# Two one-column constants in one tile: all tile pools start 32 bytes lower in a two-layer fp32 trunk

## The chip, the core and the metric

The kernel runs on one core of one Trainium2 chip. The metric is the device time of one execution in microseconds (us), the median of the runs that are shown. All tensors are float32, and the matrix products are made from float32 operands split into two parts.

## What is computed

The reference is a decoder trunk of `DEPTH` = 2 layers over 256 tokens of width 1024. Each layer has three blocks, and each block ends in a layer norm:

```
x = layer_norm(ALPHA * x + 0.5 * swiglu(x, ffn_w1[l, 0], ffn_w2[l, 0]), ...)
mix = hybrid_mixer(x, w_in[l], ...)
x = layer_norm(ALPHA * x + mix, ...)
x = layer_norm(ALPHA * x + 0.5 * swiglu(x, ffn_w1[l, 1], ffn_w2[l, 1]), ...)
```

`swiglu` is `(silu(x @ w1_gate) * (x @ w1_up)) @ w2` with an inner width of 2816. `hybrid_mixer` makes one projection of x to seven blocks of 1024 columns, runs a gated short convolution and a gated linear recurrence on them, projects each of the two results with a 1024 x 1024 matrix, merges them with sigmoid gates and projects the sum once more. Two places need a constant that an instruction reads as a one-column operand: a square root in the recurrence (a bias of 1e-30) and the power -0.5 in the layer norm.

## The kernel before

**Matrix products.** Each weight arrives in units of 128 partitions x 2048 float32 columns (1 MB). `emit_unit` (L185 to L199) loads a unit into a `raw` tile with DMAs from SyncE's queue (L193), ScalarE rounds it to `hi` (L197), and VectorE makes `lo = raw - hi` (L198). Activations are split in the same way. A product is then three matmuls: high by high, high by low and low by high, all issued in `mm` (L202). There are 8,838 matmuls with as many weight loads. In TensorE's terms, the *stationary* operand (128 columns) is loaded ahead of a matmul by a weight load, and the *moving* operand (256 or 512 columns) is streamed through. The weight load of one matmul overlaps the matmul before it.

**Which operand comes from where.** This decides what the change moves, so here are the three kinds of matmul:

- 256 columns, moving operand in the tiles of x or y, stationary operand in a weight unit. `mm_cols` (L204 to L211) makes them: the gate and up projections of the feed-forward blocks (bank `gu`), the mixer's projections (`c`, `v`, `b`, `y`, `ga`, `gb`) from `xh` and `xl`, and the two output projections (`wc`, `wr`) from `yh` and `yl`.
- 512 columns, moving operand in a weight unit, stationary operand in `xh`/`xl` (the `fill` matmuls of `filler`, L304 to L314) or in `yh`/`yl` (part of the `acc` matmuls of `form_b`, L278 to L287).
- Both operands in tiles of a pool: the other `acc` matmuls (stationary operand in an activation slot; 512 columns, but 256 in the last half of the last block), and the `rg` matmuls (256 columns, L471 to L476).

**Where the tiles lie.** A tile takes the same range of bytes in every partition. The pool `const` comes first and is as large as the sum of its tiles; the pools `praw`, `phi`, `plo`, `act` and `small` follow. In `const`, after `ident` and `xtok`, lie `xh`, `xl`, `yh` and `yl` (8 rows of 256 float32: 8,192 bytes each), `gB` and `bB` (4,096 each), `vec` (832), `hbm` and `hrg` (128 each), `sp2` (64), `tiny` and `mhalf` (one column of 4 bytes, for which 32 bytes are set aside each), then `rows0` and `rows1` (512 each) and six tiles of the parameter set-up (64 each). The tiles of the weight pools take 8,192 bytes and those of `act` 2,048 bytes. Slices of these tiles that a matmul reads begin at multiples of 512 bytes inside them.

**Order of work.** The program is a list of steps made up front (L224 to L227) and issued by the loop at L603 to L616. Ahead of each step it emits weight units as long as no more than `LOOK` = 6 are outstanding beyond those freed. The two constants are written by VectorE at L597 and L598, ahead of everything else on that engine. `mhalf` is read by GpSimd at L260, once in each of the 12 layer norms; `tiny` is read by ScalarE at L501, eight times in the kernel.

Of the kernel before, what the change touches and what calls it, by code (L numbers as in the profile page):

```python
# [9 lines left out]
F32 = mybir.dt.float32  # L10
# [4 lines left out]
P = 128  # L15
# [23 lines left out]
def trunk_kernel(  # L39
# [33 lines left out]
    const = ctx.enter_context(tc.tile_pool(name="const", bufs=1))  # L73
# [29 lines left out]
    hbm = const.tile([P, DEPTH, 2 * KD], F32, name="hbm")  # L103
    hrg = const.tile([P, DEPTH, 2 * KD], F32, name="hrg")
    sp2 = const.tile([P, DEPTH, KD], F32, name="sp2")
    tiny = const.tile([P, 1], F32, name="tiny")

    mhalf = const.tile([P, 1], F32, name="mhalf")

    def load_x(hh):  # L110
        for t in range(NT):
# [534 lines left out]
```

## Time and profile before

| what | value |
|---|---|
| median of 3 runs (lowest to highest) | 1224.68 us (1224.0 to 1225.43) |
| the profiled execution's own time | 1224.83 us |
| its span in the profile | 1223.0 us |
| granted TensorE clock, mean | 0.999 |
| VectorE busy | 825.3 us (67%) |
| ScalarE busy | 591.1 us (48%) |
| GpSimd busy | 14.9 us (1%) |
| share of the 16 DMA engines that the weight queue took | 58.6% |

A row of the profile names the engine, the line of the kernel and the tiles (out<-in, without buffer numbers). PE is a matmul on TensorE, PEld a weight load, DVE is VectorE, ACT ScalarE, POOL GpSimd, and SPq the DMA-issuing queue of SyncE. Matmuls are pipelined, so the duration of one matmul is longer than the time from its start to the start of the next; the rate is read from starts, or from the length of a run of back-to-back matmuls divided by their count. The chain of waits is the work that ended last, followed back from the end, and in it a row has the start in us, the length in us and the count.

### The profile page before, as it was taken

What the parts mean: (1) busy time and instruction counts of PE and PEld (TensorE: products, weight loads), DVE (VectorE), ACT (ScalarE), POOL (GpSimd) and SP (SyncE); (2) the same over time, 40 slices, a digit from 0 to 9 for tenths busy, and PEclk for the clock granted to TensorE, in tenths of its full rate; (3) what the DMA queues carried; (4) which work ended last, traced back from release to release, by engine and by line L of the source; (5) the groups of instructions that cost most, each with busy time, mean ns of one, the idle gap of its engine ahead of it and who ended that gap; (6) DMA issues with size and microseconds to landing.
All of it is one profiled execution on the core that took longest, in us unless ns stands there. A gap on an engine that the chain in (4) does not pass through costs nothing.

```text
span 1223.0 us, 20210 instructions
## 1 busy us (share of the span) xinstructions
PE 1207.2 (99%) x8838; PEld 1132.5 (93%) x8838; DVE 825.3 (67%) x794; ACT 591.1 (48%) x572; POOL 14.9 (1%) x20
## 2 busy tenths in 40 slices
PE   7999999999999999999999999999999999999997
PEld 5999988999999889998889998889999998899996
DVE  5766546868997785654575654577699967756533
ACT  5544434576575354443254443265856743544420
POOL 0000000000000000000000000000000000000000
PEclk9999999999999999999999999999999999999999
DMA  9975555638565566565566555565475654755610
GB/s 314 290 228 205 181 198 172 222 121 264 188 203 178 170 224 211 188 205 176 168 223 211 187 206 175 170 224 189 141 250 196 201 179 154 259 185 195 202 40 35
DMA packets 184257, 236.30 MB, mean 193 GB/s; under 512 B 4248, under 2 KB 164200, under 8 KB 184168
## 3 DMA queue, kind: packets, MB, share of 16 engines
q1 hardware_dynamic: 184168, 235.00, 58.6%
q8 instruction: 69, 1.13, 0.4%
q14 instruction: 20, 0.16, 0.0%
HBM read 233.94 MB, written 1.05 MB: 192 GB/s over the span
## 4 chain that ended last, share of the span: by engine, by line
PE 98%; DVE 1%; ACT 0%; DMA 0%; issue 0%; SPq 0%; DVEq 0%; ACTq 0%
PE gu L202 32%; PE acc L202 23%; PE fill L202 11%; PE c L202 4%; PE v L202 4%; PE b L202 4%; PE wr L202 4%; PE gb L202 4%; PE y L202 4%; PE ga L202 4%; PE wc L202 4%; PE rg L202 2%; PE xT L237 1%; DMA raw<-in_ffn_w_dram 0%; PE x L420 0%; PE hT L361 0%
## 5 line engine op out<-in xcount | busy, mean ns | idle before, releaser
L198 DVE TENSOR_TENSOR lo<-raw,hi 128x2048 fp32r<-128x2048 f32 (+1 forms) x218 | 493.8, 2270 | 254.9 <-ACT hi L197 254.6
L197 ACT CAST hi<-raw 128x2048 fp32r<-128x2048 f32 (+1 forms) x216 | 410.1, 1906 | 413.1 <-issue 190.7
L202 PE MATMUL gu<-xh,hi 128*128 128x256 f32 x1152 | 154.8, 277 | 0.0
L202 PE MATMUL gu<-xh,lo 128*128 128x256 f32 x1152 | 154.3, 276 | 0.0
L202 PE MATMUL gu<-xl,hi 128*128 128x256 f32 x1152 | 154.3, 276 | 0.0
L202 PEld LDWEIGHTS gu<-xh,hi 128*128 128x128 f32 x1152 | 141.9, 188 | 0.3
L202 PEld LDWEIGHTS gu<-xl,hi 128*128 128x128 f32 x1152 | 141.6, 188 | 0.0
L202 PEld LDWEIGHTS gu<-xh,lo 128*128 128x128 f32 x1152 | 141.5, 188 | 0.0
L202 PE MATMUL acc<-hi,hl 128*128 128x512 f32 (+1 forms) x180 | 65.8, 366 | 0.0
L202 PE MATMUL acc<-hi,hh 128*128 128x512 f32 (+1 forms) x180 | 65.8, 366 | 0.0
L202 PE MATMUL acc<-lo,hh 128*128 128x512 f32 (+1 forms) x180 | 65.8, 365 | 0.0
L345 DVE TENSOR_TENSOR hv<-hv,gu 128x512 f32<-128x512 f32 x36 | 24.8, 688 | 48.9 <-PE gu L202 48.8
L202 PE MATMUL fill<-hi,xh 128*128 128x512 f32 x192 | 53.7, 403 | 3.4 <-DVE hi L197 2.1
L202 PE MATMUL fill<-hi,xl 128*128 128x512 f32 x192 | 52.8, 398 | 0.6 <-DVE xl L242 0.6
L202 PE MATMUL acc<-hi,yh 128*128 128x512 f32 (+1 forms) x144 | 53.0, 368 | 0.0
L202 PE MATMUL acc<-hi,yl 128*128 128x512 f32 (+1 forms) x144 | 52.9, 368 | 0.0
L202 PE MATMUL fill<-lo,xh 128*128 128x512 f32 x192 | 52.6, 396 | 0.0
L202 PE MATMUL acc<-lo,yh 128*128 128x512 f32 (+1 forms) x144 | 52.4, 364 | 0.0
L202 PEld LDWEIGHTS fill<-hi,xh 128*128 128x128 f32 x192 | 36.0, 192 | 13.3 <-ACT xh L241 4.4
L202 PEld LDWEIGHTS fill<-hi,xl 128*128 128x128 f32 x192 | 36.5, 191 | 9.2 <-DVE xl L242 1.4
L202 PEld LDWEIGHTS fill<-lo,xh 128*128 128x128 f32 x192 | 36.6, 191 | 8.1
L241 ACT CAST xh<-xT 128x512 fp32r<-128x512 f32 x24 | 13.5, 590 | 60.4 <-PE xT L237 60.0
(172 smaller groups left out, 1866.4 us busy)
## 6 DMA issues: line engine op xcount, KB each, us to landing
raw<-in_ffn_w_dram SPq DMA_DIRECT2D x116, 1024.0 KB, 5.1
raw<-in_w_in_dram SPq DMA_DIRECT2D x56, 1024.0 KB, 5.1
raw<-in_ffn_w_dram SPq DMA_DIRECT2D x28, 512.0 KB, 4.1
raw<-in_w_out_conv_dram SPq DMA_DIRECT2D x8, 1024.0 KB, 5.4
raw<-in_w_out_rnn_dram SPq DMA_DIRECT2D x8, 1024.0 KB, 5.3
raw<-in_w_o_dram SPq DMA_DIRECT2D x8, 1024.0 KB, 4.9
raw<-in_rg_w_dram SPq DMA_DIRECT2D x4, 1024.0 KB, 6.6
gB<-in_ln_g_dram SPq DMA_DIRECT2D x6, 512.0 KB, 5.6
```

The lines of the kernel that those rows point to most:

```text
L197: (nc.vector.tensor_copy if first else nc.scalar.copy)(hi[:, part], raw[:, part])
L198: nc.vector.tensor_sub(lo[:, part], raw[:, part], f(hi[:, part]))
L202: nc.tensor.matmul(ps, lhs, rhs, start=first, stop=last)
L237: nc.tensor.transpose(ps[:, i * P : (i + 1) * P], xtok[:, t, c * P : (c + 1) * P], ident)
L241: nc.scalar.copy(dh, v)
L345: nc.vector.tensor_mul(o, o, u)
```

## The change

The tiles `tiny` and `mhalf` become the two columns of one tile, `two`. The names `tiny` and `mhalf` now stand for one column each, and all instructions that write or read them stay as they are.

```diff
@@ -103,9 +103,8 @@
     hbm = const.tile([P, DEPTH, 2 * KD], F32, name="hbm")
     hrg = const.tile([P, DEPTH, 2 * KD], F32, name="hrg")
     sp2 = const.tile([P, DEPTH, KD], F32, name="sp2")
-    tiny = const.tile([P, 1], F32, name="tiny")
-
-    mhalf = const.tile([P, 1], F32, name="mhalf")
+    two = const.tile([P, 2], F32, name="two")
+    tiny, mhalf = two[:, 0:1], two[:, 1:2]
```

One tile of 8 bytes takes 32 bytes where two tiles took 64. So `const` is 32 bytes smaller, and what lies behind these tiles moves down by 32 bytes: the tiles `rows0`, `rows1` and those of the parameter set-up, and all tiles of the pools. `ident`, `xtok`, `xh`, `xl`, `yh`, `yl`, `gB`, `bB`, `vec`, `hbm`, `hrg` and `sp2` stay where they are. The program has the same instructions with the same shapes on the same engines in the same order.

## The prediction

> **What bounds the kernel now.** I read the page's busy times first, then the chain of waits, then who made TensorE wait.
>
> ```profile
> span 1223.0 us, 20210 instructions
> PE 1207.2 (99%) x8838; PEld 1132.5 (93%) x8838; DVE 825.3 (67%) x794; ACT 591.1 (48%) x572; POOL 14.9 (1%) x20
> ...
> PEclk9999999999999999999999999999999999999999
> ...
> PE 98%; DVE 1%; ACT 0%; DMA 0%; issue 0%; SPq 0%; DVEq 0%; ACTq 0%
> ```
>
> The chain is 98% matmuls, at a granted clock that never drops. The list of waits, for TensorE alone:
>
> ```profile
> PE xT L237 <- DMA xtok<-in_x_dram: 4.4, 1, 4.4
> PE fill L202 <- DVE hi L197: 2.1, 2, 1.4
> PE fill L202 <- ACT xh L241: 1.3, 5, 0.3
> PE fill L202 <- DVE xl L242: 0.6, 1, 0.6
> ```
>
> These are 8.4 us in all, 4.4 of them the first load of x. So only one thing can move the time by much: the interval from one matmul to the next. The chain in order of time gives it, as length by count:
>
> ```profile
> 35.56 5.65 PE gu L202 x48
> 41.22 0.87 PE hT L361 x8
> 42.09 16.97 PE gu L202 x144
> 59.24 76.20 PE gu L202 x672
> ...
> 196.76 11.01 PE fill L202 x48
> ...
> 220.63 5.66 PE c L202 x48
> ...
> 241.37 5.66 PE c L202 x48
> ...
> 304.64 21.76 PE wc L202 x192
> ...
> 821.99 5.66 PE c L202 x48
> ...
> 842.73 5.66 PE c L202 x48
> ```
>
> The reader should divide. Matmuls of 256 columns go at 21.76 us / 192 = 113.3 ns in `wc` and 76.20 / 672 = 113.4 in `gu`, but at 16.97 / 144 = 117.8 in `gu` just before, and 5.66 / 48 = 117.9 in the first `c`. They are the same instruction, shape and alignment; nothing waits. So there are at least two steady patterns of matmul and weight load, and which of them a stretch falls into depends on how it begins.
>
> The `fill` matmuls of 512 columns take 11.01 / 48 = 229.4 ns. Now three pairs of rows from the timeline of TensorE; each pair is the first and last of a run of equal matmuls:
>
> ```profile
> 136.42 0.39 PE L202 MATMUL acc<-lo,h0h 128*128 128x512 f32 x1
> ...
> 145.94 0.39 PE L202 MATMUL acc<-lo,h0h 128*128 128x512 f32 x1
> ```
>
> From start to start there are 42 matmuls: 9.52 us / 42 = 226.7 ns. Both operands are in pools.
>
> ```profile
> 176.22 0.39 PE L202 MATMUL acc<-hi,yh 128*128 128x512 f32 x1
> ...
> 178.97 0.39 PE L202 MATMUL acc<-hi,yh 128*128 128x512 f32 x1
> ```
>
> Here 12 matmuls take 2.75 us, 229.2 ns each. The stationary operand is in `yh` and `yl`, the moving one in a pool.
>
> ```profile
> 1157.43 0.28 PE L202 MATMUL acc<-lo,h0h 128*128 128x256 f32 x1
> ...
> 1159.95 0.28 PE L202 MATMUL acc<-lo,h0h 128*128 128x256 f32 x1
> ```
>
> These are 21 matmuls of 256 columns in 2.52 us: 120.0 ns each, both operands in pools. The same shape with the moving operand in a tile of x takes 113.3.
>
> **What the addresses say.** From the start of `xh` to the first weight pool lie 4 x 8,192 + 2 x 4,096 + 832 + 2 x 128 + 64 + 2 x 32 + 2 x 512 + 6 x 64 = 43,584 bytes. That is 340 x 128 + 64. All slices and pool tiles step by multiples of 128 bytes, so any operand in a pool lies 64 bytes off any operand in `xh` to `yl`, modulo 128, and two operands in pools lie 0 off each other. Thus the trace before shows two distances: at 0, 256 columns take 120.0 ns and 512 take 226.7; at 64, 256 columns take 113.3 (sometimes 117.8) and 512 take 229.2 to 229.4. The distance is what I hold responsible; operand size, engine and clock are equal in each pair. After the change the distance from x or y to a pool is 43,552 bytes, 340 x 128 + 32. Two operands in pools stay at 0. No row shows a distance of 32. This is the unknown, bounded by rows on both sides.
>
> A rule of the Trainium skill speaks against all this: in "SBUF — State Buffer", section "Who interferes with whom", TensorE has two independent read ports, one for the moving operand and one for weight loads, and never waits on anyone. By it the distance does not matter and the change is worth 0. The trace does not agree: 120.0 against 113.3 ns for one shape.
>
> **Part by part.** *The constants.* Their instructions stay:
>
> ```profile
> L597 DVE MEMSET tiny<- x1: 59/59/59, 0.8 to 0.8; 128x1 f32 x1
> ...
> L598 DVE MEMSET mhalf<- x1: 59/59/59, 0.8 to 0.8; 128x1 f32 x1
> ...
> L260 POOL TENSOR_TENSOR rs<-rs,mhalf x12: 912/917/982, 189.3 to 1217.4; 128x1 f32<-128x1 f32 x12
> ```
>
> Both writes end before 1 us, under TensorE's wait of 4.4 us for x. Afterwards the tile is only read, so a shared tile gives no reader a new wait. Cost 0; without that cover, 0.12 us.
>
> *The 256-column matmuls with x or y moving.* Their counts, by form:
>
> ```profile
> L202 PE MATMUL gu<-xh,hi 128*128 128x256 f32 x1152 | 154.8, 277 | 0.0
> ...
> L202 PE MATMUL c<-xh,hi 128*128 128x256 f32 x128 | 17.8, 281 | 0.0
> ```
>
> `mm_cols` makes three forms of each, and the mixer has eight kinds like `c` with 128 of each form: 3 x 1,152 + 8 x 3 x 128 = 6,528 matmuls, about 740 us, over half the kernel. Upper bound: all go at the 120.0 of distance 0. About 384 already go at 117.8 (48 + 144 at the first `gu`, and four stretches of 48 `c`, by the rows of the chain above). So it is 6,144 x 6.7 + 384 x 2.2 = 42 us. At 117.8 for all it is 6,144 x 4.5 = 27.6 us. Lower bound: the 384 settle at 113.3, which gives -1.7 us. Below 113.3 I know no row of this shape, and 256 against 512 columns in their best patterns, 113.3 against 226.7, scale exactly with the columns: this looks like the stream's own rate, not a collision. I take 0. My reason is that a matmul at distance 64 has already found a pattern without loss, and half of the shift away from it need not lose it; but 32 lies as near to 0 as to 64, so this is weakly held.
>
> *The 512-column matmuls with x or y stationary.*
>
> ```profile
> L202 PE MATMUL fill<-hi,xh 128*128 128x512 f32 x192 | 53.7, 403 | 3.4 <-DVE hi L197 2.1 <-ACT xh L241 1.3
> ...
> L202 PE MATMUL acc<-hi,yh 128*128 128x512 f32 x112 | 44.1, 394 | 0.0
> ```
>
> Three forms of each: 576 + 336 = 912. At the distance-0 rate they would give back 576 x 2.7 + 336 x 2.5 = 2.4 us; at today's rate 0. A worse pattern, say as much again as today's loss, costs 2.4. Halfway between the two known distances I take half of the gain, -1.2 us.
>
> *Pool with pool.* The distance stays 0: cost 0. These operands also move by 32 bytes themselves, but so far a run follows the distance; nothing in the trace prices it.
>
> *ScalarE, VectorE and the DMAs* read and write the moved tiles.
>
> ```profile
> L198 DVE TENSOR_TENSOR lo<-raw,hi 128x2048 fp32r<-128x2048 f32 (+1 forms) x218 | 493.8, 2270 | 254.9 <-ACT hi L197 254.6
> L197 ACT CAST hi<-raw 128x2048 fp32r<-128x2048 f32 (+1 forms) x216 | 410.1, 1906 | 413.1 <-issue 190.7
> ...
> 60.00:135.00 75.00, 75.00 (x664) 75.00 (x663) 47.54 (x54) 32.81 (x30) 2.92 (x1) 1.00 0.63 211
> ...
> raw<-in_ffn_w_dram SPq DMA_DIRECT2D x116, 1024.0 KB, 5.1
> ```
>
> In 75 us of `gu`, VectorE is busy for 47.54, ScalarE for 32.81 and the DMA engines for 0.63 of the time. A unit feeds 48 matmuls, 5.44 us, against 2.27 us of subtraction. If they became 5% slower it would stay under the matmuls; uncovered are only the 4.0 us for which `fill` waits, so 0.2 us. I take 0.
>
> **Sum.** 1224.83 (the profiled execution, span 1223.0 and 1.8 around it) - 1.2 = 1223.6 us. The execution lies 0.15 above the median, which I neglect.
>
> **Rivals.**
>
> *Lost pattern (slower).* At 32 bytes off, weight loads and moving streams meet as at 0 bytes. For it: the 120.0 ns rows; the 117.8 ns stretches, which show that even at 64 the good pattern is not the only one. Against: most of the kernel holds 113.3 after many different starts. Price 42 - 2.4 (the 512 columns then go at 226.7) = 39.6: 1264.4 us; with the milder pattern 27.6: about 1252. It decides from 0.4 ns per matmul, since 6,528 x 0.38 is 2.45 us.
>
> *All patterns settle (faster).* Both small losses vanish: -2.4 - 1.7 = -4.1, 1220.7 us. For it: the 512 columns are better at 0 than at 64, so 64 is not the best distance for them. Against: at 0 the 256 columns are worst.
>
> *The stream gets faster than 113.3.* The eight `hT` transposes above take 0.87 / 8 = 109 ns each with a full weight load, so weight loads allow 109. If the change freed the stream to that rate, 6,528 x 4.3 = 28 us: 1196.8. Against: the exact scaling with columns. The Trainium skill, "TensorE: Matmul & The Clock Gate", section "Wait — 56ns, not 53.3ns?", gives columns / 2.4 GHz + 2.5 ns from start to start, an estimate of 109.2 ns for 256 columns; the trace has 113.3 at a clock of 0.999.
>
> *Nothing at all.* Independent reads, as the first rule has it: 1224.8 us. Against: the pairs of rows.
>
> **How the numbers follow.** Forecast 0.36 (1222.4 to 1226), nothing at all 0.05, lost pattern 0.33 (about half of it at the full price), all settle 0.21, a faster stream 0.05. A measurement of this kernel can tell 0.2%, 2.45 us, from no change. Faster: 0.21 + 0.05 = 0.26; within: 0.36 + 0.05 = 0.41; slower: 0.33. The range leaves out the faster stream and the last microseconds beyond the full price: 1220.0 to 1265.0. The likeliest case's own range is 1222.4 to 1226.
>
> **What would show it.** Right: `wc` stays at 21.76 us for 192 and the later `gu` at 113.4 ns; `acc` with `yh` falls between 226.7 and 229.2; the list of TensorE's waits stays near 8.4 us. A lost pattern would show as 192 `wc` in 22.6 to 23.0 us with no new wait. `fill` at 226.7 and the first `gu` at 113.3 would show that all settled. The prediction is wrong if time moves while all these intervals stand, for then it is no matter of matmul patterns.

## The result, and the profile after

The changed kernel takes 1260.4 us (median of 4 runs, 1259.39 to 1260.81) against 1225.03 us for the kernel before on the same chip: ratio 1.0281, 95% interval 1.0263 to 1.03. It is slower by 35.4 us. The span of the profiled execution grows from 1223.0 to 1259.0 us.

First the page of the changed kernel: busy times, granted clock, and the engines' shares of the chain.

```profile
span 1259.0 us, 20210 instructions
PE 1243.2 (99%) x8838; PEld 1163.9 (92%) x8838; DVE 826.0 (66%) x794; ACT 590.5 (47%) x572; POOL 14.9 (1%) x20
...
PEclk9999999999999999999999999999999999999999
...
PE 98%; DVE 1%; DMA 0%; ACT 0%; issue 0%; SPq 0%; DVEq 0%; ACTq 0%
```

The instruction counts are the same, the clock is the same, and VectorE, ScalarE and GpSimd are busy for the same time as before within 1 us. Only TensorE's busy time is longer, by 36 us, which is the whole difference of the spans. Next, the list of waits for TensorE:

```profile
PE xT L236 <- DMA xtok<-in_x_dram: 4.2, 1, 4.2
PE fill L201 <- DVE hi L196: 2.3, 2, 1.6
PE fill L201 <- ACT xh L240: 1.3, 5, 0.3
PE fill L201 <- DVE xl L241: 0.6, 1, 0.6
```

These are 8.4 us, as before: no engine and no load makes TensorE wait longer. So the time lies between matmuls that wait for nothing. The chain in order of time (start, length, count):

```profile
43.49 17.03 PE gu L201 x144
60.71 79.54 PE gu L201 x672
...
202.05 11.21 PE fill L201 x48
...
226.32 5.68 PE c L201 x48
...
312.96 22.72 PE wc L201 x192
```

Divide again. `wc` goes at 22.72 us / 192 = 118.3 ns per matmul (113.3 before), `gu` at 79.54 / 672 = 118.4 (113.4), `fill` at 11.21 / 48 = 233.5 (229.4). The first `gu` and the first `c`, which went at 117.8 and 117.9 before, go at 118.3 too. The timeline of TensorE has the other kinds, first and last row of a run:

```profile
180.64 0.40 PE L201 MATMUL acc<-hi,yh 128*128 128x512 f32 x1
...
183.44 0.40 PE L201 MATMUL acc<-hi,yh 128*128 128x512 f32 x1
...
1192.95 0.28 PE L201 MATMUL acc<-hi,h0h 128*128 128x256 f32 x1
...
1195.35 0.28 PE L201 MATMUL acc<-lo,h0h 128*128 128x256 f32 x1
```

With a stationary operand in `yh` and `yl`, 12 matmuls take 2.80 us, 233.3 ns each (229.2 before). With both operands in pools, 20 matmuls of 256 columns take 2.40 us, 120.0 ns each, as before.

The sum: 6,144 matmuls of 256 columns that went at 113.4 lose 5.0 ns, 30.7 us; the 384 others lose 0.5, 0.2 us; `fill` loses 576 x 4.2 ns, 2.4 us; `acc` on y loses 336 x 4.1, 1.4 us. The 96 `acc` matmuls of 256 columns with a stationary operand in `yh` or `yl`, in the last block, stand neither in the list of kinds above nor in the prediction's counts; they go from 113.6 to 117.4 ns on average, 0.4 us. That is 35.1 of the 36.0 us of the spans. Another 1.0 us lies in the first 20 `fill` matmuls, which follow the first loads: 7.73 us by the chain, 6.69 before. They took 7.48 in the first experiment below, where all distances are as before, so that is not shown to be an effect of the change.

### The profile page after: what moved, and what is told of

Read it like the earlier page. It is cut to its first block, busy times and chain, and to the rows that moved or that the text cites. A ratio compares the mean times of both kernels' runs of the same rounds, so it can differ in the third digit from the quotient of the medians.

```text
span 1259.0 us, 20210 instructions
## 1 busy us (share of the span) xinstructions
PE 1243.2 (99%) x8838; PEld 1163.9 (92%) x8838; DVE 826.0 (66%) x794; ACT 590.5 (47%) x572; POOL 14.9 (1%) x20
## 4 chain that ended last, share of the span: by engine, by line
PE 98%; DVE 1%; DMA 0%; ACT 0%; issue 0%; SPq 0%; DVEq 0%; ACTq 0%
PE gu L201 32%; PE acc L201 23%; PE fill L201 11%; PE c L201 4%; PE v L201 4%; PE b L201 4%; PE gb L201 4%; PE y L201 4%; PE ga L201 4%; PE wc L201 4%; PE wr L201 4%; PE rg L201 2%; PE xT L236 1%; DMA raw<-in_ffn_w_dram 0%; PE hT L360 0%; PE x L419 0%
## 5 line engine op out<-in xcount | busy, mean ns | idle before, releaser
L197 DVE TENSOR_TENSOR lo<-raw,hi 128x2048 fp32r<-128x2048 f32 (+1 forms) x218 | 493.8, 2270 | 272.3 <-ACT hi L196 272.2
L201 PE MATMUL gu<-xh,hi 128*128 128x256 f32 x1152 | 160.2, 281 | 0.0
L201 PE MATMUL gu<-xl,hi 128*128 128x256 f32 x1152 | 159.8, 281 | 0.0
L201 PE MATMUL gu<-xh,lo 128*128 128x256 f32 x1152 | 159.8, 281 | 0.0
L201 PEld LDWEIGHTS gu<-xh,hi 128*128 128x128 f32 x1152 | 146.7, 188 | 0.4
L201 PEld LDWEIGHTS gu<-xl,hi 128*128 128x128 f32 x1152 | 146.5, 188 | 0.0
L201 PEld LDWEIGHTS gu<-xh,lo 128*128 128x128 f32 x1152 | 146.5, 188 | 0.0
```

The costliest lines, as they stand in the source:

```text
L197: nc.vector.tensor_sub(lo[:, part], raw[:, part], f(hi[:, part]))
L201: nc.tensor.matmul(ps, lhs, rhs, start=first, stop=last)
```

## The experiments

From here on, the *distance* is the place of the stationary operand minus that of the moving one, in bytes of a partition, modulo 256 (the runs show below that 256 is the period). All distances are worked out from the sizes and the order of the tiles in the program; no trace here lists addresses. For the 256-column matmuls that stream x or y the distance is 64 before and 32 after. For the 512-column ones the roles are exchanged, so it is -64 (192) before and -32 (224) after. All kernels but the two that change `mm_cols` have the same instructions in the same order on every engine. The rows under each experiment are from the chain in order of time.

**Theory:** the interval of a matmul follows the distance of its own two operands. **Rivals:** the shared tile costs; or what counts is where a tile itself begins.

### Sharing without the shift

```diff
     two = const.tile([P, 2], F32, name="two")
+    gap = const.tile([P, 1], F32, name="gap")
```

> The constants share a tile, and an unused tile of 32 bytes behind it puts the pools back: distance of a pool from x and y 64 modulo 128. Distance theory: as before, 1224.7 us, wc at 113.3 ns per matmul. Rival, the shared tile itself costs (its readers or writers wait): as after, 1260 us.

Measured: 1224.73 us, ratio 0.9997 (0.9986 to 1.0009).

```profile
59.69 76.20 PE gu L202 x672
...
197.20 11.01 PE fill L202 x48
...
305.09 21.76 PE wc L202 x192
```

These three are the lengths of before to the last digit. The shared tile costs nothing; the 32 bytes account for the whole loss.

### Everything 32 bytes higher

```diff
+    gap = const.tile([P, 8], F32, name="gap")
     ident = const.tile([P, P], F32, name="ident")
```

> The kernel before with an unused tile of 32 bytes ahead of everything: x, y and all pools move up by 32 bytes, the pools now begin at 96 modulo 128 instead of 64, and the distance stays 64. Distance theory: 1224.7 us, wc at 113.3 ns. Rival, what counts is where a tile itself begins (a multiple of 64 bytes or not): 1260 us or more, since x and pools both lie 32 bytes off.

Measured: 1224.7 us, ratio 0.9998 (0.9984 to 1.0012).

```profile
196.32 11.01 PE fill L203 x48
...
304.39 21.76 PE wc L203 x192
```

Weights, slots, x and y all lie off a multiple of 64 bytes here, and nothing is lost. So 32 bytes more in the place of every operand do not matter to this kernel. That holds for the casts, the subtractions and the loads too, which work on the same moved tiles: a cast to `hi` takes 1,906 ns, a subtraction 2,270 ns and a 1 MB load of the feed-forward weights 5.1 us, in the kernel before and here.

### Pools 32, 64 and 128 bytes higher

```diff
     mhalf = const.tile([P, 1], F32, name="mhalf")
+    gap = const.tile([P, 8], F32, name="gap")    # 16 and 32 columns in the other two
```

> The kernel before with 32 bytes more ahead of the pools: distance 96 instead of 64. Distance theory: if 32 bytes more is the mirror image of 32 bytes less, as after, 118.3 ns for 256 columns and 233.3 for 512 with x or y stationary, 1260 us; if only the sense from moving to stationary counts, the two classes differ from after, and 256 columns lie between 113.3 and 120. Rival, where a tile itself begins: pools off a multiple of 64, 1260 us.

> The kernel before with 64 bytes more ahead of the pools: distance 0 modulo 128. Distance theory, by the pool-with-pool rows of before: 256 columns at 120.0 ns, 512 at 226.7, so 1264.4 us. Rival, where a tile itself begins: pools now at a multiple of 128, 1224.7 us or less.

> The kernel before with 128 bytes more ahead of the pools: distance 192 instead of 64, 64 modulo 128. Distance theory with a period of 128 bytes: as before, 1224.7 us, wc 113.3 ns and fill 229.4 ns per matmul. Rival, a longer period (512 bytes): other intervals, any time from 1222 to 1262 us.

Measured: 1258.24 us at distance 96, ratio 1.0266 (1.0244 to 1.0288); 1262.19 us at 128, ratio 1.0297 (1.0274 to 1.032); 1256.12 us at 192, ratio 1.025 (1.0235 to 1.0265). The three kernels in this order:

```profile
200.86 11.21 PE fill L203 x48
...
311.29 22.53 PE wc L203 x192
```

```profile
200.99 11.17 PE fill L203 x48
...
312.01 22.79 PE wc L203 x192
```

```profile
201.69 11.22 PE fill L203 x48
...
312.08 22.61 PE wc L203 x192
```

`wc` goes at 117.3, 118.7 and 117.8 ns, `fill` at 233.5, 232.7 and 233.8. The place of a tile is refuted once more, since at 128 and at 192 all pools begin at multiples of 64. But my own theory failed in part: I had taken 128 bytes for the period. Then 128 should have given `fill` the 226.7 of distance 0, and 192 should have been as good as 64. Neither is so.

### Distance 0, 320 and 256: the period

The first diff moves `sp2` (64 bytes) from behind the tiles of x and y to ahead of them; the second moves `hbm` and `hrg` (256 bytes), the third all three.

```diff
+    sp2 = const.tile([P, DEPTH, KD], F32, name="sp2")
     ident = const.tile([P, P], F32, name="ident")
...
-    sp2 = const.tile([P, DEPTH, KD], F32, name="sp2")
```

> The tile sp2 of 64 bytes moves ahead of everything: x and y lie 64 bytes higher, the pools stay, and the distance is 0 modulo 512 (in the run at distance 0 modulo 128 it was 128 modulo 512, and fill took 232.7 ns there, against 226.7 for two operands in pools, which lie 0 modulo 512 apart or at other multiples of 512). Period of 128 bytes: as that run, 1262 us, fill 232.7 ns, wc 118.7 ns. Rival, a period of 512 bytes: fill at 226.7 ns and wc at 120 ns, 1224.7 + 6,528 x 6.2 ns - 912 x 2.4 ns = 1263 us; so fill decides and not the time.

> hbm and hrg (128 bytes each) lie ahead of everything instead of behind the tiles of x and y, so that pools lie 256 bytes lower relative to them: distance 320 instead of 64 modulo 512. Theory of a period of 256 bytes: as before, 1225 us (wc 113.3 ns, fill 229.4). Theory of a period of 512 bytes: no such repetition; any value from the range so far, wc between 113.3 and 120, 1225 to 1265 us.

> hbm, hrg and sp2 lie ahead of everything: distance 256 modulo 512. Period of 256 bytes: as at distance 0, wc 120.0 ns and fill 226.7 to 227, 1265.6 us. Period of 512 bytes: as at 128, 96 or 192, wc 117.8 to 119.2 ns and fill 232 to 233.5, about 1256 to 1262 us.

Measured: 1265.59 us at 0, ratio 1.0331 (1.0316 to 1.0346); 1224.89 us at 320, ratio 0.9996 (0.998 to 1.0012); 1265.22 us at 256, ratio 1.0313 (1.0291 to 1.0335). In this order:

```profile
201.91 10.90 PE fill L202 x48
...
313.26 23.04 PE wc L202 x192
```

```profile
196.85 11.01 PE fill L202 x48
...
304.77 21.76 PE wc L202 x192
```

```profile
202.35 10.90 PE fill L202 x48
...
313.69 23.04 PE wc L202 x192
```

In these rows 320 equals 64, and 256 equals 0, length by length: the period is 256 bytes. At 0 `wc` takes 120.0 ns and `fill` 227.1, which are, within 0.4 ns, the values of two operands in pools in the kernel before. So at distance 0 the interval is the same, whichever tiles it lies between. At 0 the `fill` matmuls are at their best and the 256-column ones at their worst.

### 16 bytes off

```diff
-    xh = const.tile([P, KD, S], F32R, name="xh")
...
+    xy = const.tile([P, 4 * KD * S + 8], F32R, name="xy")
+    xh, xl, yh, yl = [xy[:, 4 + i * KD * S : 4 + (i + 1) * KD * S].rearrange("p (k s) -> p k s", s=S) for i in range(4)]
```

> The changed kernel with x and y in one tile, starting 16 bytes inside it: distance 48, halfway between before (64) and after (32). Theory that 64-byte lines of the two operands must begin together: anything off 64 costs as 32 does, 118.4 ns, 1258 to 1262 us. Theory that the cost grows with the distance from 64: 115.9 ns, 1242 us.

> The kernel before with x and y in one tile, starting 16 bytes inside it, and the pools 32 bytes higher: distance 80, halfway between 64 and 96. Lines that must begin together: 118.2 ns, 1256 to 1260 us. Cost that grows with the distance from 64: 115.8 ns, 1242 us.

Measured: 1263.93 us at 48, ratio 1.0302 (1.028 to 1.0323), and 1263.7 us at 80, ratio 1.0301 (1.0276 to 1.0326).

```profile
201.89 11.14 PE fill L199 x48
...
313.18 22.88 PE wc L199 x192
```

```profile
201.51 11.06 PE fill L200 x48
...
312.70 22.90 PE wc L200 x192
```

`wc` goes at 119.2 and 119.3 ns, more than either expectation had, and both times are above all the ranges expected. One rival is left here: in these two kernels alone x and y begin 16 bytes off a multiple of 32, and no run moves them by 16 bytes at a distance of 64. So the loss at 48 and 80 can be that of the distance or that of this start. A cost that grows with the distance from 64 is refuted without them: 128 bytes off (192) cost less than 64 bytes off (128), 117.8 against 118.7 ns. Among the distances tried, 64 is a single good place for `wc`, with loss on both sides.

### x at 64 and y at 32

```diff
 (on the changed kernel)
+    gap = const.tile([P, 8], F32, name="gap")
     yh = const.tile([P, KD, S], F32R, name="yh")
```

> The changed kernel with 32 unused bytes between xl and yh: x to pools 64 as before the change, y to pools 32 as after it. If each stretch follows the distance of its own two operands: gu, c and the others from x at 113.3 ns, fill at 229.4, wc and wr (768 matmuls) at 118.3, acc with y stationary (336) at 233.3: 1224.7 + 3.8 + 1.4 + 0.4 (96 of 256 columns) = 1230.3 us. Rival, one common state of the whole kernel, or the place of the pools themselves: 1224.7 or 1260 us.

Measured: 1230.25 us, ratio 1.0043 (1.0028 to 1.0058).

```profile
41.84 16.34 PE gu L202 x144
58.36 76.20 PE gu L202 x672
...
196.33 11.01 PE fill L202 x48
...
304.21 22.71 PE wc L202 x192
326.93 21.79 PE ga L202 x192
```

This is the sharpest of the tests: in one execution, `ga` streams x and takes 21.79 us; `wc`, just ahead of it and with the same weight pools, streams y and takes 22.71. Each of the two follows its own pair of operands, and the sum hits the time (1230.3 us expected). (The first 144 `gu`, at 117.8 before, go at 113.5 here, at the same distance of 64.)

### Slots 64 bytes higher

```diff
+    pgap = ctx.enter_context(tc.tile_pool(name="pgap", bufs=1))
+    gap = pgap.tile([P, 16], F32, name="gap")
     act = ctx.enter_context(tc.tile_pool(name="act", bufs=NSLOT))
```

> The kernel before with an unused 64 bytes between the weight pools and the pool of activation slots: x to weights stays 64, slots to weights 64 modulo 128 instead of 0. Own-pair distance: rg and the last acc of 256 columns (359) from 119.5 to 113.8 ns, -2.0 us; acc of 512 columns with a slot stationary (779) from 227.2 to 229.1, +1.5 us: 1224.2 us, a change in the intervals and none in the time. Rival: slots do not matter, intervals as before.

Measured: 1229.49 us, ratio 1.004 (1.0021 to 1.0058).

```profile
135.81 57.04 PE acc L204 x246
...
239.49 2.83 PE rg L204 x24
...
305.67 21.76 PE wc L204 x192
```

The rows of the kernel before to compare with:

```profile
135.44 55.97 PE acc L202 x246
...
238.07 2.86 PE rg L202 x24
```

A miss in size, and it shows that the sense counts. `acc` of 512 columns with a slot stationary now has distance +64, not the -64 of `fill`. It lost 57.04 - 55.97 = 1.07 us per 246 matmuls, far more than I had given it. `rg` has the slot moving, so -64 (192), and goes at 2.83 / 24 = 117.9 ns, not at 113.8. Both agree with the run at 192: 117.8 for 256 columns at 192, and 233.8 for 512 at +64. The `acc` of 256 columns with a slot stationary, now at +64, did what was expected: 113.5 ns on average.

But the distance and its sense do not settle the interval for every kind. In the kernel before, `acc` of 256 columns with a stationary operand in y lies at -64 (192) as well. First and last row of a run of them:

```profile
1185.30 0.28 PE L202 MATMUL acc<-hi,yh 128*128 128x256 f32 x1
...
1187.91 0.28 PE L202 MATMUL acc<-lo,yh 128*128 128x256 f32 x1
```

These 23 matmuls take 2.61 us from start to start, 113.5 ns each, where `wc` and `rg` at 192 take 117.8 and 117.9. The shape and the distance are the same. One thing that differs is the order: in `acc` the stationary operand alternates between the high and the low tile. No run separates this from other differences, so why it matters is open.

### hi at 64, lo at 96

```diff
+    pgap = ctx.enter_context(tc.tile_pool(name="pgap", bufs=1))
+    gap = pgap.tile([P, 8], F32, name="gap")
     plo = ctx.enter_context(tc.tile_pool(name="plo", bufs=NBUF))
```

> The kernel before with an unused 32 bytes between the pools phi and plo: hi lies 64 off x and y as before, lo 96. Matmuls of 256 columns come as eight xh by hi, eight xl by hi, eight xh by lo. Pair theory: the eight with lo go at about 118, the sixteen with hi at 113.3. If the partner of a stream is the weight load of the next matmul, the last of the sixteen (its successor loads lo) is slow already and the last of the eight (its successor loads hi) is fast again; if it is the matmul's own stationary operand, the other way round. Time: 2,176 x 4.8 ns = 10.4 us and some more for acc and fill, 1237 to 1243 us. Rival, the whole stretch shares one pattern: all 24 slow, 1255 us or more.

The turns, by themselves or on top of this:

```diff
         for k, ah, al in xs:
             mm(ps, u.h[:, k, c : c + P], ah, first and k == xs[0][0], False)
+            mm(ps, u.l[:, k, c : c + P], ah, False, False)
         for k, ah, al in xs:
-            mm(ps, u.h[:, k, c : c + P], al, False, False)
-        for k, ah, al in xs:
-            mm(ps, u.l[:, k, c : c + P], ah, False, last and k == xs[-1][0])
+            mm(ps, u.h[:, k, c : c + P], al, False, last and k == xs[-1][0])
```

> As the run with lo at 96, and mm_cols issues high by high and low by high in turns (hi, lo, hi, lo and so on for sixteen, then eight with hi). Own and next stationary operand then always differ in the sixteen. Next weight load as partner: matmuls on hi (a load of lo under them) slow, those on lo fast; own operand as partner: matmuls on lo slow, those on hi fast; if neither, both kinds in between, since the start of one matmul passes its shift on to the next. Time near that of the run without the turns, 1235 to 1260 us.

> The kernel before with the same turns in mm_cols and all distances as before (hi and lo 64 off x and y): the control for the turns. Pair theory: order does not matter, 113.3 ns, 1224.7 us. Rival, the turns themselves cost: over 1230 us.

Measured: 1247.88 us with lo at 96, ratio 1.0108 (1.0072 to 1.0144); 1256.69 us with the turns on top, ratio 1.0176 (1.014 to 1.0212); 1235.75 us with the turns alone. In this group of runs the kernel before itself spread from 1224.68 to 1239.74 us at an equal clock, and the control with the turns from 1228.18 to 1239.29 (its ratio is 1.0007, 0.9973 to 1.004). So I read the intervals and leave the differences of a few us alone. The control's trace, of an execution of 1228.18 us, shows where such a spread can come from:

```profile
460.16 92.50 PE gu L202 x816
...
643.88 96.11 PE gu L202 x816
```

One of its long `gu` stretches goes at 117.8 ns and the others at 113.4, at the same distance of 64, which is 3.6 us. The kernel has four such stretches (three of 816 matmuls, and one of 144 and 672), and the times of the kernel before in this group lie near steps of this size (1224.68, 1228.13, 1232.8, 1236.0, 1239.74 us); those executions were not traced, so that each step is such a stretch is not shown.

The timeline of TensorE with lo at 96, in groups of eight:

```profile
499.98 1.07 PE L204 MATMUL gu<-xl,hi 128*128 128x256 f32 x8
500.89 1.12 PE L204 MATMUL gu<-xh,lo 128*128 128x256 f32 x8
501.86 1.08 PE L204 MATMUL gu<-xh,hi 128*128 128x256 f32 x8
502.77 1.07 PE L204 MATMUL gu<-xl,hi 128*128 128x256 f32 x8
```

From start to start, eight matmuls on hi take 0.91 us and eight on lo 0.97 us, so 114 and 121 ns, in turns: the pattern follows the operands within a few matmuls. So a stretch does not share one pattern, but the time met neither expectation: lo at 96 goes at 120 ns here and not at 118, and `acc` loses as well (57.19 us for 246). Worked out from the starts of all such groups in the trace: the last of the sixteen on hi, under which the first lo is loaded, takes 117.6 ns on average (288 of them), against 113.8 for one between two others on hi. No lo is yet its own operand, so the loss begins one matmul ahead, at the time of the next weight load. But the last of the eight on lo, under which a hi is loaded, still takes 120.1 (273), and the next two 116.6 and 115.7. The return takes a few matmuls. That is half of what either form of the theory expected. With the turns and lo at 96, all places in the sixteen lie between 114 and 124 ns in no plain order, so that run decides nothing. The control alone is as before: its chain has `wc` at

```profile
304.04 21.76 PE wc L202 x192
```

## Why the prediction was wrong

*What bounds the kernel* held: the matmul interval is all that moved, and waits and other engines stayed as they were. *The constants, ScalarE, VectorE and the DMAs* at 0 held, shown by the two runs that keep the distance (1224.73 and 1224.7 us). *Pool with pool* at 0 held: 120.0 ns before and after for 256 columns, and 227.1 and 227.8 on average for 512.

*The step that failed* is the one on the 256-column matmuls, where I took 0 because "a matmul at distance 64 has already found a pattern without loss, and half of the shift away from it need not lose it". It lost 5.0 ns in 6,144 matmuls, 30.7 us. Nothing in the trace of before spoke for this step; the rows there bounded it by -1.7 and 42 us, and I chose the good end. The runs show why the choice was bad: of the distances tried, these matmuls reach 113.3 at 64 only, and 0, 32, 48, 80, 96, 128 and 192 give 117.3 to 120.0. (The values at 48 and 80, and those at 208 and 176 in the second table, hold with x and y 16 bytes off, as said above. The row is that of `wc`; at 96 `gu` goes at 118.7.)

| distance, modulo 256 | 0 | 32 | 48 | 64 | 80 | 96 | 128 | 192 |
|---|---|---|---|---|---|---|---|---|
| `wc`, 256 columns, ns | 120.0 | 118.3 | 119.2 | 113.3 | 119.3 | 117.3 | 118.7 | 117.8 |

*The 512-column matmuls* were mis-sized and of the wrong sign: -1.2 us forecast by halving between two known distances, +3.8 us measured. Their row, by their own distance (the negative of the one above), from `fill` in the same runs:

| distance, modulo 256 | 0 | 224 | 208 | 192 | 176 | 160 | 128 | 64 |
|---|---|---|---|---|---|---|---|---|
| `fill`, 512 columns, ns | 227.1 | 233.5 | 232.1 | 229.4 | 230.4 | 233.5 | 232.7 | 233.8 |

Halving between two points of such a curve means nothing. Behind both lies *what the addresses say*: two distances modulo 128 were all that I read in the trace, and I took them for the whole law. The period is 256, so what I called 64 were two distances, 64 for the 256 columns and 192 for the 512, and the sense counts for most kinds.

*The rival of the lost pattern* was right in place and sign: `wc` came at 22.72 us with no new wait, inside the 22.6 to 23.0 it had named, and the 256 columns lost 30.7 us against its 27.6 to 42. Its reason, that 32 acts as 0 does, is not borne out in full: 118.3 ns is not the 120.0 of distance 0, and the 512 columns lost where it had them gain 2.4 us. *All patterns settle*, *the stream gets faster* and *nothing at all* are refuted: `gu`, `c` and `wc` go at 118.3 to 118.4 and `fill` at 233.5. The rule of the Trainium skill, "SBUF — State Buffer", section "Who interferes with whom", that TensorE's two reads are independent and wait on no one, does not describe these runs: 32 bytes of distance cost 2.8%.

What stays open is the mechanism below the distance. Shown is that the change costs what it costs through the distance of the pools from x and y: the time came back with the 32 bytes, 32 bytes more in all places changed nothing, and within one execution `wc` and `ga` went each by their own distance. Not shown is a law that gives the interval from the distance alone: at 192 one kind takes 113.5 ns and two others 117.8 and 117.9. That the weight load of the next matmul and the moving stream disturb each other's reads is argued from the border between hi and lo, which told one side only. Also open is why stretches at one distance sometimes change their pace: `gu` at 64 between 113.4 and 117.8 ns, and `fill` in the run with the slots moved between 11.00 and 11.21 us for 48.

No version tried is faster than the kernel before. Among the distances tried, 64 is best for the 256-column matmuls that stream x or y, of which this kernel has 6,528, and 0 for the 512-column ones, of which 912 are concerned.

## What to carry to other kernels

When TensorE is the bound and waits for nothing, divide the length of runs of matmuls by their count and compare equal shapes: unequal intervals at an equal clock are a finding. Then work out where their operands lie, modulo 256 bytes, against each other, since a constant tile added or merged anywhere ahead of a pool can change it. Treat an untried distance as a risk, here of up to 3.3% of the time between the best and the worst one tried, and time it; do not interpolate.

## What the runs showed of the hardware that was not expected

- In this kernel, matmuls of 256 float32 columns, back to back with their weight loads, go at 113.3 to 120.0 ns according to the distance of stationary and moving operand modulo 256 bytes; those of 512 columns at 226.7 to 233.8.
- Moving all operands together does not matter: 32 bytes more for all of them left `wc` at 21.76 us and `fill` at 11.01.
- One distance can have two steady patterns: at 64, the same 144 `gu` took 16.97 us in the kernel before and 16.34 us where only y had another distance, and of two equal stretches of 816 `gu` in one execution one took 92.50 us and the other 96.11.
- The same distance does not mean the same interval for every kind: at 192, 256 columns take 113.5 ns in `acc` and 117.8 in `wc`.
